# First FFN products of a hybrid encoder trunk taken slice by slice of the depth in eight PSUM banks, with new planned TensorE durations

## The chip, the cores and the metric

The kernel runs on one core of one Trainium2 chip. The metric is the time of one execution on the device in microseconds (us), lower is better. Engines are TensorE (PE; PEld is its weight load), VectorE (DVE), ScalarE (ACT), GpSimd (POOL) and SyncE (SP), which issues nearly all transfers.

## What is computed

A trunk of two layers, one sequence of 256 tokens of width 1024, all in float32. Each layer, with shift, scale and gate of every sub-layer computed from a vector c:

```python
x += 0.5 * g1 * SwiGLU(mod1(RMSNorm(x)))     # FFN 1
h  = mod2(RMSNorm(x)); p = h @ W_in
x += g2 * W_out(sum_b sigmoid(p_gate_b) * (mixer_b(p) @ P_b))   # three token mixers
x += 0.5 * g3 * SwiGLU(mod3(RMSNorm(x)))     # FFN 2

def modulate(h, shift, scale):
    return h * (1 + scale[:, None, :]) + shift[:, None, :]
def swiglu(h, wi, wo):
    gate, up = jnp.split(h @ wi, 2, axis=-1)
    return (jax.nn.silu(gate) * up) @ wo
```

Shift, scale and gate of all nine kinds are c (after SiLU) times `ada_w`, plus `ada_b`. The mixers are a dilated window attention, a 2-D neighbourhood attention and an RWKV-7 scan in both directions. The FFN is 2816 wide, 22 column blocks of 128 for the gate and 22 for the up half.

## The kernel before

Activations lie transposed, channels on the 128 partitions in eight slices (k = 0 to 7, `KT` = 8) and 256 tokens along the free axis. A float32 product is made from three float32r ones (`mm3`, lines 395 to 398): weights and activations are split into a high part (a cast, on ScalarE for weights) and a low part (the difference, on VectorE), and TensorE adds high x high, high x low and low x high in one PSUM bank.

**Who sets the order.** All instructions are written by a planner (`Order`, line 58). The stages are generators that say `yield on(engine, duration)`, `wait(event)` or `take(semaphore)`; the planner runs them in planned time, always the request that can start first, with a priority among equals. The order in which they come out is the order of each engine's queue on the chip. Planned durations are constants in the code: `MM` = 0.329 us for a triple of dense matmuls, 0.615 for eight small 64x64 ones, 1.14 for the reduction of an `ada_w` block, 1.45 for a transfer's issue. Buffers are counted too: `s_big` for 32 tiles of 4 KiB a partition, `s_pm` and `s_px` for 3 and 5 of the eight PSUM banks. The planner also models TensorE's clock (`clock`, line 103).

**The main stream.** `weights`, `weights_hi` and `weights_lo` (lines 331 to 364) load the weights in their order of use, 512 KB at a time, and split them in quarters; `dense` (line 440) runs the products. In `ffn` (line 785) each column block j takes gate and up (s = 0, 1) over all eight k, then `ffn_evac` (line 643) makes z on ScalarE and VectorE. Behind the first products, `ada` (line 492) loads further `ada_w` blocks at a planned pace (`FPACE` = 5 us from `FSTART` = 12 us on) and `ada_block` (line 457) reduces each against c on VectorE (line 460).

**The start.** The first sub-layer cannot use the main stream at once: its h needs the scale and the shift, eight `ada_w` blocks each, and the sum of squares of x. `first_loads` (line 721) loads, in the order of the list `FIRST`, `ada_w` blocks and halves of the weights of the first six column blocks (`NJ0` = 6; one half holds four k of one block, in runs of 2 KiB). The scale blocks are reduced on VectorE. The shift blocks of slices 0 to 6 are multiplied by c on GpSimd and added up on ScalarE (`first_shift`, line 697):

```python
nc.gpsimd.tensor_tensor(out=raw, in0=raw, in1=csb, op=OP.mult)
S_.activation(raw, raw, AF.Copy, scale=0.5, accum_out=modT[0][:, k:k + 1])
```

`first_put` (line 736) makes a slice of h: x times the reciprocal norm on VectorE, scale and shift on ScalarE, the cast on ScalarE, the low part on VectorE. `first_products` (line 756) takes six PSUM banks at once and runs the products in the order in which h and weight halves come, two k-halves a block. Then the other 16 column blocks follow from the main stream.

**After it.** The token mixer works with `ORDER` = "cabAgB": projections, the RWKV chain (inversion steps pX, pT at lines 1175 and 1186, the scan with pU at line 1296), the attentions, gates. The chains' small matmuls stand between dense ones; a chain's result `oC` (line 1435) is the last branch of the mixer. The columns of shift that `Stats.scale` (lines 511 to 527) writes are needed by the first products of the next sub-layer (`pearly`).

Of the kernel before, what the change touches and what calls it, by code (L numbers as in the profile page):

```python
# [16 lines left out]
KT = D // 128  # L17
# [12 lines left out]
NJ0, SHV = 6, (7,)  # L30
FIRST = ((0,), (0, 0), (1, 0), (2, 0), (3, 0), (4, 0), (1,), (5, 0), (2,), (0, 1), (1, 1), (3,), (2, 1), (3, 1), (4,), (4, 1), (5,), (5, 1), (6,), (7,))
# [4 lines left out]
LAT, MM = {"PE": 0.2, "ACT": 0.15, "DVE": 0.13, "SP": 0.0}, 0.329  # L36
# [21 lines left out]
class Order:  # L58
# [6 lines left out]
    def __init__(self):  # L65
        self.threads, self.free, self.cur, self.n = [], {}, None, 0
        self.dense, self.cols, self.thin, self.row, self.tab = None, {}, 0.0, 0, None

# [48 lines left out]
    def run(self):  # L117
        while self.threads:
# [11 lines left out]
            if kind == "on":  # L130
# [8 lines left out]
                if a == "PE":  # L139
                    if th is self.dense:  # L140
                        self.row += 1
                        if self.row >= BURST:
                            self.thin = 0.0
                    else:
                        self.row = 0
                        self.thin += b
                    b = self.clock(t, b, 0.98 if th is self.dense else 0.6) - t
# [11 lines left out]
def on(eng, dur, lat=None, tab=None):  # L159
    return ("on", eng, dur, LAT[eng if isinstance(eng, str) else eng[0]] if lat is None else lat, tab)  # L160
# [27 lines left out]
def trunk(ctx, tc, A, out):  # L188
# [404 lines left out]
    def rstd(st):  # L593
# [4 lines left out]
        yield on("PE", 0.6)  # L598
# [83 lines left out]
    w0 = {(j, q): Event() for j in range(NJ0) for q in range(2)}  # L682
    raws0 = {q: Event() for q in w0}

    def first_weights(j, q, raw):
        yield take(s_big, 2)
        hi, lo = (big("w0" + n, (128, 2, 512), F32R) for n in "hl")
        yield wait(raws0[j, q])
# [5 lines left out]
        w0[j, q].w = hi, lo  # L694
        od.set(w0[j, q])

    def first_shift(k, raw, got):
        yield wait(got)
        yield on("POOL", 2.3, 0.2)
        nc.gpsimd.tensor_tensor(out=raw, in0=raw, in1=csb, op=OP.mult)  # L700
        yield on("ACT", 1.05)
        S_.activation(raw, raw, AF.Copy, scale=0.5, accum_out=modT[0][:, k:k + 1])
        free_big()
        yield on("DVE", 0.07)
        V.tensor_add(modT[0][:, k:k + 1], modT[0][:, k:k + 1], ada_b[:, 0, k:k + 1])
        od.set(have1[k])

    def first_mod(k):
        if k in SHV:
            yield from ada_load(0, k, 1, False)  # L710
            yield from ada_load(0, 8 + k, 1, False)
            return
        yield take(s_big)
        raw, got = big("raw0", (128, D)), Event()
        yield on("SP", 1.45, 0.0)
        nc.sync.dma_start(raw, A["ada_w"][0, k])
        od.set(got, 2.0)
        od.spawn(first_shift(k, raw, got), 1)
        yield from ada_load(0, 8 + k, 1, False)

    def first_loads():

        for x in FIRST:
            if len(x) == 1:
                yield from first_mod(x[0])
                continue
            j, q = x
            yield take(s_big)
            raw = big("w0raw", (128, 2, 512))
# [26 lines left out]
    def first_products(ha):  # L756

        sems = [s_px] * min(NJ0, 4) + [s_pm] * (NJ0 - 4)
        for q in sems:
            yield take(q)  # L760
        ps0, za = [paux("pfirst", (128, 2, 256)) for _ in range(NJ0)], None
        at_ = {tuple(x): i for i, x in enumerate(FIRST)}
        jobs = sorted((max(at_[k,], at_[j, k // 4]), k, j) for k in range(KT) for j in range(NJ0))
        n, left0 = [0] * NJ0, [4 * NJ0] * 2
        for _, k, j in jobs:
            n[j] += 1
            if k == KT - 1 and za is None:
# [12 lines left out]
            left0[k // 4] -= 1  # L780
# [1127 lines left out]
```

## Time and profile before

| | us |
|---|---|
| median of three runs | 1587.9 |
| lowest, highest | 1582.06, 1589.01 |
| profiled execution, its own time | 1586.35 |
| its span, first to last instruction | 1584.6 |
| mean granted TensorE clock | 0.985 |

The profile is of one execution. Busy times of matmuls overlap, as each is counted until its result is written, so how far TensorE is from its peak is read from the distance of starts. A row of the timeline holds the start, the length, the engine, the line, what is written from what, the shape and, in brackets, the engine's idle time before it with what ended it; "x6" merges six like instructions. A row of the waits says who waited for what, then the total, the number of times and the longest. The granted clock is given as a share of 2.4 GHz.

### The profile page before, as it was taken

What the parts mean: (1) busy time and instruction counts of PE and PEld (TensorE: products, weight loads), DVE (VectorE), ACT (ScalarE), POOL (GpSimd) and SP (SyncE); (2) the same over time, 40 slices, a digit from 0 to 9 for tenths busy, and PEclk for the clock granted to TensorE, in tenths of its full rate; (3) what the DMA queues carried; (4) which work ended last, traced back from release to release, by engine and by line L of the source; (5) the groups of instructions that cost most, each with busy time, mean ns of one, the idle gap of its engine ahead of it and who ended that gap; (6) DMA issues with size and microseconds to landing.
All of it is one profiled execution on the core that took longest, in us unless ns stands there. A gap on an engine that the chain in (4) does not pass through costs nothing.

```text
span 1584.6 us, 36797 instructions
## 1 busy us (share of the span) xinstructions
PE 1533.1 (97%) x14518; PEld 1450.6 (92%) x14518; DVE 1311.7 (83%) x2938; ACT 897.0 (57%) x1854; POOL 21.3 (1%) x29
## 2 busy tenths in 40 slices
PE   3999999999999989999999999999999999999998
PEld 3999999988888889999999999998888987999997
DVE  7878889989888869997779877898888896888664
ACT  4655567576554447554565545676655445565554
POOL 3100000000000000000000000000000000000000
PEclk7999999999999989999999999999999999899999
DMA  8588864545464225888657876544446422467553
GB/s 310 188 293 272 284 230 163 180 130 198 140 230 140 74 80 174 277 287 273 226 200 272 285 266 203 185 159 155 160 159 232 168 102 68 136 202 274 184 184 127
DMA packets 91621, 311.61 MB, mean 197 GB/s; under 512 B 11444, under 2 KB 14772, under 8 KB 91448
## 3 DMA queue, kind: packets, MB, share of 16 engines
q1 hardware_dynamic: 91160, 309.15, 57.8%
q8 instruction: 114, 1.87, 0.5%
q14 instruction: 59, 0.48, 0.1%
q10 hardware_dynamic: 288, 0.10, 0.0%
HBM read 308.17 MB, written 1.05 MB: 195 GB/s over the span
## 4 chain that ended last, share of the span: by engine, by line
PE 88%; DMA 5%; DVE 4%; issue 1%; ACT 1%; SPq 0%; DVEq 0%; ACTq 0%
PE pmain L396 21%; PE pmain L397 20%; PE pmain L398 20%; DMA araw<-in_ada_w_dram 5%; PE pearly L396 2%; PE pearly L398 2%; PE pearly L397 2%; PE pX L1175 2%; PE pT L1186 2%; PE pG L1158 1%; PE pS L1488 1%; PE po L1528 1%; DVE wlo L361 1%; PE pmain L1645 1%; PE pmain L1647 1%
## 5 line engine op out<-in xcount | busy, mean ns | idle before, releaser
L352 ACT CAST whi<-wraw 128x512 fp32r<-128x512 f32 x836 | 511.9, 619 | 427.3 <-PE pmain L397 256.0
L361 DVE TENSOR_TENSOR wlo<-wraw,whi 128x512 fp32r<-128x512 f32 x836 | 571.7, 688 | 118.7 <-ACT whi L352 109.2
L396 PE MATMUL pmain<-h,whi 128*128 128x256 f32 x1872 | 539.2, 288 | 0.0
L398 PE MATMUL pmain<-h,wlo 128*128 128x256 f32 x1872 | 525.2, 281 | 1.1 <-DVE wlo L361 1.1
L397 PE MATMUL pmain<-h,whi 128*128 128x256 f32 x1872 | 525.2, 281 | 0.0
L396 PEld LDWEIGHTS pmain<-h,whi 128*128 128x128 f32 x1872 | 351.7, 188 | 13.3 <-issue 4.6
L398 PEld LDWEIGHTS pmain<-h,wlo 128*128 128x128 f32 x1872 | 352.2, 188 | 1.6 <-DVE wlo L361 1.6
L397 PEld LDWEIGHTS pmain<-h,whi 128*128 128x128 f32 x1872 | 352.3, 188 | 0.4
L460 DVE CUSTOM_DVE_ANT_0 araw<-araw,csb 128x1024 f32<-128x1024 f32 x137 | 169.0, 1235 | 47.6 <-DMA araw<-in_ada_w_dram 47.2
L398 PE MATMUL pmain<-z,wlo 128*128 128x256 f32 x704 | 198.2, 282 | 3.4 <-DVE wlo L361 3.3
L397 PE MATMUL pmain<-z,whi 128*128 128x256 f32 x704 | 197.9, 281 | 0.0
L396 PE MATMUL pmain<-z,whi 128*128 128x256 f32 x704 | 197.8, 281 | 0.0
L398 PEld LDWEIGHTS pmain<-z,wlo 128*128 128x128 f32 x704 | 132.6, 188 | 4.4 <-DVE wlo L361 4.2
L396 PEld LDWEIGHTS pmain<-z,whi 128*128 128x128 f32 x704 | 132.6, 188 | 0.0
L397 PEld LDWEIGHTS pmain<-z,whi 128*128 128x128 f32 x704 | 132.6, 188 | 0.0
L396 PE MATMUL pearly<-xh,whi 128*128 128x258 f32 x320 | 91.4, 286 | 0.0
L398 PE MATMUL pearly<-xh,wlo 128*128 128x258 f32 x320 | 90.4, 282 | 0.0
L397 PE MATMUL pearly<-xl,whi 128*128 128x258 f32 x320 | 90.2, 282 | 0.0
L397 PEld LDWEIGHTS pearly<-xl,whi 128*128 128x128 f32 x320 | 60.6, 189 | 0.0
L396 PEld LDWEIGHTS pearly<-xh,whi 128*128 128x128 f32 x320 | 60.4, 189 | 0.0
L398 PEld LDWEIGHTS pearly<-xh,wlo 128*128 128x128 f32 x320 | 60.3, 189 | 0.0
L419 ACT CAST z<-ffz 128x256 fp32r<-128x256 f32 x76 | 30.7, 405 | 40.3 <-DVE ffz L651 39.9
(306 smaller groups left out, 2459.2 us busy)
## 6 DMA issues: line engine op xcount, KB each, us to landing
wraw<-in_ffn_wi_dram SPq DMA_DIRECT2D x164, 512.0 KB, 4.9
araw<-in_ada_w_dram SPq DMA_DIRECT2D x137, 512.0 KB, 6.4
wraw<-in_ffn_wo_dram SPq DMA_DIRECT2D x88, 512.0 KB, 4.5
wraw<-in_w_in_dram SPq DMA_DIRECT2D x78, 512.0 KB, 3.7
wraw<-in_w_gb_dram SPq DMA_DIRECT2D x72, 512.0 KB, 4.2
wraw<-in_w_out_dram SPq DMA_DIRECT2D x16, 512.0 KB, 3.6
w0raw<-in_ffn_wi_dram SPq DMA_DIRECT2D x12, 512.0 KB, 9.8
raw<-in_ada_w_dram SPq DMA_DIRECT2D x7, 512.0 KB, 7.9
```

Source lines behind the costliest of these rows:

```text
L352: S_.copy(hi, part(q))
L361: V.tensor_tensor(lo, part(q), hi, op=OP.subtract)
L396: P.matmul(o, w[0], xh, start=first, stop=False)
L397: P.matmul(o, w[0], xl, start=False, stop=False)
L398: P.matmul(o, w[1], xh, start=False, stop=last)
L419: S_.copy(self.hi(k), src)
L460: V.tensor_tensor_reduce(out=raw, in0=raw, in1=csb, scale=0.5, scalar=0.0, op0=OP.mult, op1=OP.add, accum_out=modT[l][:, blk:blk + 1])
L1158: P.matmul(pp[b][:, i], BK[d][i // 2][hs, i % 2, c].rearrange("p a b -> p (a b)"), ar_view(d, i // 2)[hs, :, i % 2, cs_], start=True, stop ...
L1175: P.matmul(px[half(h), h // 2], G[half(h), h // 2, h % 2, 0:64], T[half(h), h // 2], start=True, stop=True)
L1186: P.matmul(pt[half(h), h // 2], X[half(h), h // 2], TT[half(h), h // 2], start=True, stop=True)
L1488: P.matmul(pS[e][:, t], qT[half(e), hp, t * 128:(t + 1) * 128], kT[half(e), hp], start=True, stop=True)
L1528: P.matmul(po[half(e)], vv[:, j, (2 * hp + e) * 64:(2 * hp + e + 1) * 64], pt_[:, 2 * e + j], start=j == 0, stop=j == 1)
```

## The change

`NJ0` becomes 8, and `FIRST`, `first_shift` and `first_mod` go. `first_loads` now goes by slices: for each k the scale block and the shift block, both reduced on VectorE through `ada_load`, and for each pair of slices four weight pieces, each with two k of four column blocks of one half (gate or up), in runs of 1 KiB. A piece takes three large buffers when it is issued. `first_put` waits for the scale first and makes x times scale times norm in one VectorE step, then adds the shift with the cast on ScalarE, and makes the low part with a three-operand VectorE step. `first_products` runs k by k, for each k over all eight blocks, with all eight banks open until the last k. In the planner a triple takes 0.354 instead of 0.329 us, the small steps get other durations and a form, and a change of form on TensorE costs `TURN` = 0.2 us. No instruction outside the start is added or removed; the order in every queue is planned anew.

```diff
--- before.py
+++ after.py
@@ -27,13 +27,13 @@
-NJ0, SHV = 6, (7,)
-FIRST = ((0,), (0, 0), (1, 0), (2, 0), (3, 0), (4, 0), (1,), (5, 0), (2,), (0, 1), (1, 1), (3,), (2, 1), (3, 1), (4,), (4, 1), (5,), (5, 1), (6,), (7,))
+NJ0 = 8
...
-LAT, MM = {"PE": 0.2, "ACT": 0.15, "DVE": 0.13, "SP": 0.0}, 0.329
+LAT, MM = {"PE": 0.2, "ACT": 0.15, "DVE": 0.13, "SP": 0.0}, 0.354
+TURN = 0.2
@@ -137,6 +138,9 @@ Order.run
                 if a == "PE":
+                    if th.req[5] != self.form:
+                        self.form = th.req[5]
+                        b += TURN
@@ -679,71 +684,52 @@
         yield from za.put(j, z)
         od.release(s_z, 3)
 
-    w0 = {(j, q): Event() for j in range(NJ0) for q in range(2)}
+
+
+    w0 = {(g, i): Event() for g in range(KT // 2) for i in range(NJ0 // 2)}
     raws0 = {q: Event() for q in w0}
 
-    def first_weights(j, q, raw):
-        yield take(s_big, 2)
-        hi, lo = (big("w0" + n, (128, 2, 512), F32R) for n in "hl")
-        yield wait(raws0[j, q])
+    def first_weights(g, i, raw):
+        hi, lo = (big("w0" + n, (128, 1024), F32R) for n in "hl")
+        yield wait(raws0[g, i])
         yield on("ACT", 0.94)
         S_.copy(hi, raw)
         yield on("DVE", 1.13)
         V.tensor_tensor(lo, raw, hi, op=OP.subtract)
         free_big()
-        w0[j, q].w = hi, lo
-        od.set(w0[j, q])
-
-    def first_shift(k, raw, got):
-        yield wait(got)
-        yield on("POOL", 2.3, 0.2)
-        nc.gpsimd.tensor_tensor(out=raw, in0=raw, in1=csb, op=OP.mult)
-        yield on("ACT", 1.05)
-        S_.activation(raw, raw, AF.Copy, scale=0.5, accum_out=modT[0][:, k:k + 1])
-        free_big()
-        yield on("DVE", 0.07)
-        V.tensor_add(modT[0][:, k:k + 1], modT[0][:, k:k + 1], ada_b[:, 0, k:k + 1])
-        od.set(have1[k])
-
-    def first_mod(k):
-        if k in SHV:
-            yield from ada_load(0, k, 1, False)
-            yield from ada_load(0, 8 + k, 1, False)
-            return
-        yield take(s_big)
-        raw, got = big("raw0", (128, D)), Event()
-        yield on("SP", 1.45, 0.0)
-        nc.sync.dma_start(raw, A["ada_w"][0, k])
-        od.set(got, 2.0)
-        od.spawn(first_shift(k, raw, got), 1)
-        yield from ada_load(0, 8 + k, 1, False)
+        w0[g, i].w = tuple(t.rearrange("p (j k c) -> p j k c", j=4, k=2) for t in (hi, lo))
+        od.set(w0[g, i])
 
     def first_loads():
 
-        for x in FIRST:
-            if len(x) == 1:
-                yield from first_mod(x[0])
-                continue
-            j, q = x
-            yield take(s_big)
-            raw = big("w0raw", (128, 2, 512))
-            yield on("SP", 1.45, 0.0)
-            nc.sync.dma_start(raw, A["ffn_wi"][0, 0, j].rearrange("p (s q c) -> p s q c", s=2, q=2)[:, :, q])
-            od.set(raws0[j, q], 2.0)
-            od.spawn(first_weights(j, q, raw), 2)
+        for k in range(KT):
+            yield from ada_load(0, 8 + k, 0, False)
+            yield from ada_load(0, k, 0, False)
+            for i in range(0 if k % 2 else NJ0 // 2):
+                yield take(s_big, 3)
+                raw = big("w0raw", (128, 1024))
+                yield on("SP", 1.45, 0.0)
+                j0, c0 = i // 2 * 4, i % 2 * 1024 + 128 * k
+                nc.sync.dma_start(raw.rearrange("p (j c) -> p j c", j=4),
+                                  A["ffn_wi"][0, 0, j0:j0 + 4].rearrange("j p c -> p j c")[:, :, c0:c0 + 256])
+                od.set(raws0[k // 2, i], 2.0)
+                od.spawn(first_weights(k // 2, i, raw), 2)
         od.set(e_w)
 
     def first_put(k, ha):
+        yield wait(have1[8 + k])
         yield take(s_z)
         t = small("ht")
-        yield on("DVE", 0.34)
-        V.tensor_mul(t, xT[:, k], first.r)
-        yield wait(have1[8 + k])
+        yield on("DVE", 0.4)
+        V.scalar_tensor_tensor(t, xT[:, k], modT[0][:, 8 + k:9 + k], first.r, op0=OP.mult, op1=OP.mult)
         yield wait(have1[k])
+        sh = modT[0][:, k:k + 1]
         yield on("ACT", 0.4)
-        S_.activation(t, t, AF.Identity, scale=modT[0][:, 8 + k:9 + k], bias=modT[0][:, k:k + 1])
-        yield from ha.put(k, t)
+        S_.activation(ha.hi(k), t, AF.Identity, bias=sh)
+        yield on("DVE", 0.396)
+        V.scalar_tensor_tensor(ha.lo(k), t, sh, ha.hi(k), op0=OP.add, op1=OP.subtract)
         od.release(s_z)
+        od.set(ha.ev[k])
@@ -754,32 +740,28 @@
         first.used()
 
     def first_products(ha):
-
-        sems = [s_px] * min(NJ0, 4) + [s_pm] * (NJ0 - 4)
-        for q in sems:
-            yield take(q)
-        ps0, za = [paux("pfirst", (128, 2, 256)) for _ in range(NJ0)], None
-        at_ = {tuple(x): i for i, x in enumerate(FIRST)}
-        jobs = sorted((max(at_[k,], at_[j, k // 4]), k, j) for k in range(KT) for j in range(NJ0))
-        n, left0 = [0] * NJ0, [4 * NJ0] * 2
-        for _, k, j in jobs:
-            n[j] += 1
-            if k == KT - 1 and za is None:
+        sems = [s_pm] * NPM + [s_px] * (NJ0 - NPM)
+        ps0, za = [], None
+        for k in range(KT):
+            if k == KT - 1:
                 yield take(s_big, 12)
                 za = Act("z", NJ)
-            yield wait(w0[j, k // 4])
-            hi, lo = w0[j, k // 4].w
-            for s in range(2):
-                c = slice(k % 4 * 128, k % 4 * 128 + 128)
-                if ha.ev[k].t is None or ha.ev[k].t > od.cur.t:
-                    yield wait(ha.ev[k])
-                yield on("PE", MM, 0.0)
-                mm3(ps0[j][:, s], (hi[:, s, c], lo[:, s, c]), ha.hi(k), ha.lo(k), n[j] == 1 and s == 0, n[j] == KT and s == 1)
-            if n[j] == KT:
-                od.spawn(ffn_evac(j, ps0[j], za, sems[j]), 1)
-            left0[k // 4] -= 1
-            if left0[k // 4] == 0:
-                free_big(2 * NJ0)
+            for i in range(NJ0 // 2):
+                yield wait(w0[k // 2, i])
+                hi, lo = w0[k // 2, i].w
+                for j in range(i // 2 * 4, i // 2 * 4 + 4):
+                    if ha.ev[k].t is None or ha.ev[k].t > od.cur.t:
+                        yield wait(ha.ev[k])
+                    if k == 0 and i % 2 == 0:
+                        yield take(sems[j])
+                        ps0.append(paux("pfirst", (128, 2, 256)))
+                    yield on("PE", MM, 0.0)
+                    mm3(ps0[j][:, i % 2], (hi[:, j % 4, k % 2], lo[:, j % 4, k % 2]), ha.hi(k), ha.lo(k),
+                        k == 0 and i % 2 == 0, k == KT - 1 and i % 2 == 1)
+                    if k == KT - 1 and i % 2 == 1:
+                        od.spawn(ffn_evac(j, ps0[j], za, sems[j]), 1)
+                if k % 2 == 1:
+                    free_big(2)
         return za
...
-            yield on("PE", 0.86)
+            yield on("PE", 0.86, form="64x128")
...
-                    yield on("PE", 0.435, 0.2 if i == 3 else 0.0)
+                    yield on("PE", 0.22, 0.2 if i == 3 else 0.0, form="64x128")
...
-                    yield on("PE", 0.615)
+                    yield on("PE", 0.48, form="64x64")
...
-                yield on("PE", 0.96)
+                yield on("PE", 0.87, form="64x128")
...
-                    yield on("PE", 0.65, 0.0)
+                    yield on("PE", 0.7, 0.0)
...
```

## Rows read from the trace of the kernel before

**Rows 1.** The page's first part: busy time, share of the span and instructions.
```profile
PE 1533.1 (97%) x14518; PEld 1450.6 (92%) x14518; DVE 1311.7 (83%) x2938; ACT 897.0 (57%) x1854; POOL 21.3 (1%) x29
```
**Rows 2.** Windows of 10 us: stretch, length, busy by engine, clock, DMA share, GB/s.
```profile
10.00:20.00 10.00, 2.56 (x10) 2.07 (x10) 8.10 (x12) 5.45 (x8) 3.05 (x2) 0.53 1.04 394
20.00:30.00 10.00, 3.26 (x13) 2.97 (x14) 10.00 (x12) 3.83 (x6) 6.07 (x3) 0.50 1.04 398
30.00:40.00 10.00, 6.53 (x39) 5.93 (x38) 9.58 (x13) 4.72 (x8) 3.00 (x2) 0.84 0.49 170
```
**Rows 3.** Waits of TensorE, 0 to 60 us: total us, times, longest.
```profile
PE pfirst L396 <- ACT h L419: 9.5, 2, 6.8
```
**Rows 4.** Timeline of all engines, 0 to 45 us: start, length, engine, line.
```profile
8.24 5.01 DVE L566 TENSOR_TENSOR sqacc<-sqacc,sq 128x256 f32<-128x256 f32 x6
...
9.00 2.38 POOL L700 TENSOR_TENSOR raw<-raw,csb 128x1024 f32<-128x1024 f32 x1 [8.57 <-DMA raw<-in_ada_w_dram]
...
27.52 3.13 POOL L700 TENSOR_TENSOR raw<-raw,csb 128x1024 f32<-128x1024 f32 x1 [2.68 <-DMA raw<-in_ada_w_dram]
...
28.32 3.41 DVE L460 CUSTOM_DVE_ANT_0 araw<-araw,csb 128x1024 f32<-128x1024 f32 x1
```
**Rows 5.** Timeline of VectorE, 36 to 51 us, away from GpSimd.
```profile
36.66 1.22 DVE L460 CUSTOM_DVE_ANT_0 araw<-araw,csb 128x1024 f32<-128x1024 f32 x1
...
38.06 0.15 DVE L705 TENSOR_TENSOR modT<-modT,c_ada_b 128x1 f32<-128x1 f32 x1
...
49.07 1.22 DVE L692 TENSOR_TENSOR w0l<-w0raw,w0h 128x1024 fp32r<-128x1024 f32 x1
50.26 0.43 DVE L421 TENSOR_TENSOR h<-ht,h 128x256 fp32r<-128x256 f32 x1
50.60 1.22 DVE L460 CUSTOM_DVE_ANT_0 araw<-araw,csb 128x1024 f32<-128x1024 f32 x1
```
**Rows 6.** Timeline of TensorE: runs of first products, then the first streamed product.
```profile
28.34 0.41 PE L398 MATMUL pfirst<-h,w0l 128*128 128x256 f32 x1
...
30.90 0.37 PE L398 MATMUL pfirst<-h,w0l 128*128 128x256 f32 x1
...
50.18 0.28 PE L396 MATMUL pfirst<-h,w0h 128*128 128x256 f32 x1
...
55.13 0.28 PE L396 MATMUL pfirst<-h,w0h 128*128 128x256 f32 x1
...
69.12 0.28 PE L396 MATMUL pmain<-h,whi 128*128 128x256 f32 x1
```
**Rows 7.** Timelines, 217 to 225 us: last shift column written, first product that uses it.
```profile
217.06 0.17 DVE L526 TENSOR_TENSOR xl<-modT,xh 128x8 fp32r<-128x8 f32 x1
...
224.32 0.28 PE L396 MATMUL pearly<-xh,whi 128*128 128x258 f32 x1
```
**Rows 8.** Waits of TensorE from 60 us to the end: total us, times, longest.
```profile
PE pgi L1408 <- DVE gsq L1403: 3.2, 2, 1.6
PE pmain L396 <- ACT oC L1435: 2.8, 2, 1.4
PE pvar L1390 <- ACT gsq L1382: 2.3, 2, 1.1
```
**Rows 9.** One window at the end of the first layer's token mixer, columns as in rows 2.
```profile
573.80:584.10 10.30, 7.58 (x31) 6.75 (x32) 5.16 (x13) 2.82 (x7) 0.00 (x0) 0.50 0.00 0
```
**Rows 10.** Groups of TensorE instructions by form: count, busy us, mean ns, idle before.
```profile
L1175 PE MATMUL pX<-txw,G 64*64 64x64 f32 x768 | 32.4, 223 | 1.6 <-DVE txw L1238 1.4
L1186 PE MATMUL pT<-txw 64*64 64x64 f32 x768 | 32.3, 223 | 0.0
```
**Rows 11.** Timeline of TensorE around one small step among dense matmuls, 566 us.
```profile
566.56 0.28 PE L398 MATMUL pmain<-h,wlo 128*128 128x256 f32 x1
566.77 0.68 PE L1296 MATMUL pU<-txw 64*64 64x64 f32 x16
...
567.60 0.28 PE L397 MATMUL pmain<-o,whi 128*128 128x256 f32 x1
```

More of the change, by code (lines that the diff above doesn't have):

```diff
@@ L67, in __init__ @@
         self.dense, self.cols, self.thin, self.row, self.tab = None, {}, 0.0, 0, None
+        self.form = None
     def spawn(self, gen, prio, dense=False):
@@ L155, in run, with on @@
             self.step(th)
-def on(eng, dur, lat=None, tab=None):
-    return ("on", eng, dur, LAT[eng if isinstance(eng, str) else eng[0]] if lat is None else lat, tab)
+def on(eng, dur, lat=None, tab=None, form=None):
+    return ("on", eng, dur, LAT[eng if isinstance(eng, str) else eng[0]] if lat is None else lat, tab, form)
 def wait(ev):
@@ L597, in rstd @@
         p = paux("pss")
-        yield on("PE", 0.6)
+        yield on("PE", 0.9)
         for t in range(2):
@@ L1026, in kk_norm @@
                     pss = paux("pkk", (128, S))
-                yield on("PE", 0.5)
+                yield on("PE", 0.44, form="128x32")
                 head_sum(pss, d, kq, d == 1)
@@ L1061, in finish @@
                     p = paux("pinv", (128, 2, S))
-                    yield on("PE", 0.434)
+                    yield on("PE", 0.48, form="64x128")
                     head_bcast(p, d, q, KK)
@@ L1103, in finish @@
                     pbs = paux("pbs", (128, S))
-                yield on("PE", 0.5)
+                yield on("PE", 0.44, form="128x32")
                 head_sum(pbs, d, RKV[d, 1], d == 1)
@@ L1119, in finish @@
                     p = paux("pbon", (128, 2, S))
-                    yield on("PE", 0.434)
+                    yield on("PE", 0.48, form="64x128")
                     head_bcast(p, d, q, rows)
@@ L1183, in invert @@
                     pt = paux("pT", (128, 4, 64))
-                    yield on("PE", 0.615)
+                    yield on("PE", 0.48, form="64x64")
                     for h in range(8):
@@ L1246, in values @@
                 p = paux("pBT", (128, 4, 64))
-                yield on("PE", 0.22)
+                yield on("PE", 0.25, form="64x128")
                 for i in range(4):
@@ L1254, in values @@
             p = paux("pvt", (128, 4, 64))
-            yield on("PE", 0.648)
+            yield on("PE", 0.48, form="64x64")
             for h in range(8):
@@ L1263, in values @@
             p = paux("pMV", (128, 4, 64))
-            yield on("PE", 0.615)
+            yield on("PE", 0.48, form="64x64")
             for h in range(8):
@@ L1285, in scan @@
                     p = paux("pAS", (128, 4, 64))
-                    yield on("PE", 0.615)
+                    yield on("PE", 0.48, form="64x64")
                     for h in range(8):
@@ L1293, in scan @@
                 p = paux("pU", (128, 4, 64))
-                yield on("PE", 0.615)
+                yield on("PE", 0.48, form="64x64")
                 for h in range(8):
@@ L1305, in scan @@
                     p = paux("pS1", (128, 4, 64))
-                    yield on("PE", 0.615)
+                    yield on("PE", 0.48, form="128x64")
                     for h in range(8):
@@ L1321, in scan @@
                 p = paux("pY", (128, 4, 64))
-                yield on("PE", 1.275 if ST is not None else 0.615)
+                yield on("PE", 1.05 if ST is not None else 0.48, form="128x64")
                 for h in range(8):
@@ L1387, in post @@
             p = paux("pvar", (128, 8))
-            yield on("PE", 0.8)
+            yield on("PE", 0.9)
             for hp in range(4):
@@ L1524, in attend @@
                 po = paux("po", (128, S))
-                yield on("PE", 0.96)
+                yield on("PE", 0.87, form="128x64")
                 for j in range(2):
```

## Prediction

> **What bounds the kernel now.** I read the share of each engine first: TensorE holds matmuls for 97% of the span, the next engine (VectorE) 83% [rows 1]. So a gain must either give TensorE back idle time or time at the low clock; work taken from another engine is worth nothing by itself. Next I looked at where TensorE is not full. The stretches of the first 40 us show it busy for 2.6, 3.3 and 6.5 of 10 us, at a granted clock of 0.53, 0.50 and 0.84, while VectorE is busy for 8.1, 10.0 and 9.6 [rows 2]; 0.50 is the lower of the clock's two levels, 1.2 of 2.4 GHz. In the waits of that stretch the biggest one is the first product waiting for a slice of h, 9.5 us in two pieces [rows 3]. So the start is bound by VectorE, and the rows say why: whenever GpSimd multiplies an `ada_w` block by c, a VectorE instruction beside it grows. The reduction of line 460 takes 3.41 us beside a GpSimd product and 1.22 us alone [rows 4, 5]; six additions of squares take 5.01 us with one GpSimd product of 2.38 us over them [rows 4].
>
> The first products end and the streamed ones begin at 69.12 us [rows 6]. From there TensorE is almost never short: the nine lines of its waits behind that point add up to about 21 us, and three of them belong to the end of the token mixer, with 3.2, 2.8 and 2.3 us [rows 8].
>
> **The start, part by part.** *Matmuls.* Nothing is added or dropped: eight of the 22 column blocks of the first FFN product go in the first part instead of six, and 14 instead of 16 are streamed. At the high clock 42 starts in a row take 55.13 - 50.18 = 4.95 us, 0.118 us each; at the low one 12 starts take 30.90 - 28.34 = 2.56 us, 0.213 us each [rows 6]. A streamed block is 16 x 3 = 48 matmuls, 5.66 us. Before, the first FFN product ends at about 69.1 + 16 x 5.66 = 159.7 us. After, it ends at T + 14 x 5.66 = T + 79.2, where T is the end of the first part. The change therefore gains 80.5 - T, and T has to be found.
>
> *GpSimd out, VectorE in.* Seven GpSimd products and seven ScalarE reductions go; all 16 `ada_w` blocks are reduced on VectorE. A block costs 38.06 - 36.66 = 1.40 us from its start to the next instruction but one, its small corrections included [rows 5]. Sixteen of them are 22.4 us, of which about seven, 9.8 us, are new on VectorE; what goes with GpSimd is the blocking. Low parts of the weight pieces: 50.26 - 49.07 = 1.19 us each [rows 5], 16 pieces instead of 12, 19.0 us. Two small steps for each of the eight slices: one takes 50.60 - 50.26 = 0.34 us now [rows 5]; the new forms read one operand more, and I take 0.40 us, an estimate, so 6.4 us. VectorE starts this after the squares: without GpSimd 8.24 + 5.01 - 2.38 = 10.9 us [rows 4]. Then 10.9 + 22.4 + 19.0 + 6.4 = 58.7 us if it never waits. In 10 to 40 us it was idle for 2.3 us [rows 2]; I add that, 61.0 us. The last slice is then ready and TensorE needs 48 x 0.118 = 5.7 us for it: T = 66.7, rounded to 67.
>
> *TensorE beside it.* 8 x 48 = 384 matmuls are 45.3 us at the high clock. VectorE needs (58.7 - 10.9) / 8 = 6.0 us for a slice, TensorE 5.7 us, so the slices follow each other almost without idle time, and TensorE ends just behind VectorE. If the first slice starts about 17 us (10.9 plus two reductions and two or three weight pieces), TensorE alone would end at 62.3 us, some 2 us later with a low clock at the beginning. It is no second bound, but it is close. The products of a slice wait in TensorE's order for that slice of h and its weight pieces; only later slices are queued behind them, and nobody else needs TensorE there.
>
> *Loads.* 32 pieces of 0.524 MB and x of 1.05 MB are 17.8 MB; at the 394 to 398 GB/s of 10 to 30 us [rows 2] that is 45 us, against 61 us of VectorE. They are hidden as long as space for them comes free: each weight piece now takes three of the 32 large buffers at its issue, and a pair of slices gives its eight back only when TensorE has used the second one. Before, DMA fell to 170 GB/s in 30 to 40 us [rows 2] because buffers were full; this can come again. A weight piece comes in runs of 1 KiB instead of 2 KiB, which no row shows. From below that costs nothing (pieces of 2 and of 4 KiB runs share the full rate); from above, if a run cost the same time whatever its size, a piece would take 2.6 us instead of 1.3, 16 x 1.3 = 21 us more. I take nothing, the row being nearer; the other end is a rival. SP issues nothing else in this stretch, so no other queue is delayed by the new order; the streamed weights queue behind these loads as they did.
>
> *Banks.* All eight PSUM banks are held until the last slice. The streamed product waits for bank 0 of them, which is emptied while the second half of the last slice (2.8 us) still runs on TensorE; its chain of one ScalarE and two VectorE steps of about 0.4 us each [rows 5] fits. If VectorE is behind then, up to 2 us show; that is inside the range.
>
> *What is late next.* The shift columns for the early products of the mixer are ready at 217.2 us and first used at 224.3 us, 7.1 us later [rows 7]. The use moves forward by 13 us. Their loads are paced in planned time, 24 blocks in steps of 5 us beginning 12 us behind T; planned time ran fast before (a triple was planned at 0.329 us and takes 3 x 0.118 = 0.354), so 127 planned us were 137 real ones. With 0.354 they come 10 us earlier besides the 2 us of T. About 5 us of cover stay: I cost it at nothing, and at 4 us if the pace doesn't move.
>
> So the start gains 80.5 - 67 = 13.5 us; I book 13.
>
> **The rest of the order.** No instruction changes there; the order of each queue is made anew. Dense triples are planned 7.6% longer. An excursion to small matmuls, the 16 of pU, takes from the dense matmul before it (566.56) to the second one after it (567.60) 1.04 us, less two dense starts 0.80 us [rows 11]; it was planned at 0.615 and is now 0.48 + 0.2 + 0.2 = 0.88. So the plan was optimistic for TensorE everywhere, and its chains through VectorE and ScalarE were covered with more dense work than they needed. That shows twice: few waits within the mixer, and a mixer chain that ends after the dense work has run out, with idle time and a clock of 0.50 for 10.3 us [rows 8, 9]. With true durations less dense work stands between two steps of a chain; the chain ends earlier, but has less cover. At most the end is worth its idle time, (3.2 + 2.8 + 2.3) / 2 = 4.2 us, and half of the other 6.1 us at the low clock, 3 us, or 7.2 us in each of two layers, about 14 us. I take about a fifth of that, 3 us, because thinner cover takes some back, and VectorE, the next engine [rows 1], does not get faster.
>
> **Sum.** The profiled execution took 1586.35 us (span 1584.6): 1586.35 - 13 - 3 = 1570.4, say 1570. It lies 1.6 us under the median of 1587.9 us, inside the spread of the three runs, so the same figure stands against the median. About 0.5% (7.9 us) is what a measurement here tells from no change: faster means under 1580.0, slower over 1595.8.
>
> **Rivals.** *Low clock, the slower end.* Slices come at VectorE's pace; if TensorE stays at 0.213 us a start for the whole part, it takes 384 x 0.213 = 82 us from 17 us on, T = 99, a loss of 18.5 us: 1586.35 + 18.5 - 3 = 1602. It decides from T = 80.5, that is if 141 of the 384 starts or more run low beyond what I booked (13.5 / 0.095). Against it: a TensorE at half speed is never idle here, since 10.2 us a slice exceeds VectorE's 6.0, and in the trace the start went from 0.213 to 0.118 us after an unbroken run of low starts [rows 6]. For it: the clock there is 0.50 in 20 to 30 us [rows 2], so the part begins low. The Trainium skill, "TensorE: Matmul & The Clock Gate", section "HAM oscillation — how this bites in real kernels", speaks against the change here: a loop that waits for new data at each K tile makes the array go back to its low clock at each of them. By that rule the result is this rival's; the row bears it out only in part, as the low clock is there but ended under unbroken work. Chance 0.07.
>
> *The loads.* With the upper price of the 1 KiB runs, or the same lost to full buffers, the loads end 21 us later, about 71 us, and T is near 80: the start gains nothing, 1583. For it speaks the fall to 170 GB/s [rows 2]; against it that the loads need 45 of the 61 us, so that some 13 us may be lost before they decide. Chance 0.14.
>
> *Thin cover.* pX and pT alone are 768 matmuls each, 16 to a step: 96 steps of the inversion chain [rows 10]. If TensorE now waits 0.3 us at each, that is 29 us: 1586.35 - 13 + 29 = 1602; from 0.14 us a step it eats the start's gain. Against it: VectorE's planned costs are near its real ones (a weight piece 1.13 us planned, 1.19 real), so the cover should just do. Chance 0.14.
>
> *The mixer's end goes too.* All 14 us of it: 1586.35 - 13 - 14 = 1559. Chance 0.13.
>
> **Chances and range.** My forecast has the remaining 0.52, with a range of its own of 1561 to 1579. Faster: 0.50 of it, all of the last rival, and a few hundredths of the loads and of thin cover, 0.67. Slower: the low clock and half of thin cover with a rest of the forecast, 0.15. The same: 0.18. The range leaves out the far ends of thin cover and the low clock above and little below: 1556 to 1592.
>
> **What would show it.** Right: no GpSimd product; line 460 never over 1.3 us in the first 65 us; first streamed product between 64 and 70 us; each slice's 48 matmuls close behind the one before. Wrong: starts of 0.213 us behind 30 us (low clock); TensorE or ScalarE waiting for a weight load in 20 to 60 us (loads); waits of TensorE for VectorE in 240 to 560 us well above now; or the first early product of the mixer waiting for the shift columns. The end of the mixer without a stretch at 0.50 would show that more was won than I book.

## The result and the profile after

The changed kernel takes 1594.41 us (median of 8 runs, 1588.43 to 1599.34), the kernel before 1584.74 us (8 runs, 1581.3 to 1589.01): a ratio of 1.0061, with an interval of 1.0037 to 1.0084. It is slower by some 0.6%, where 1570 was forecast. The profiled execution took 1599.34 us (span 1597.6), 4.9 us above the median; that of before took 1586.35. The two are 13.0 us apart, 3.3 more than the medians, and what is summed from the traces below is larger by that.

The page's first part, as in [rows 1]:

```profile
PE 1540.4 (96%) x14518; PEld 1453.6 (91%) x14518; DVE 1308.3 (82%) x2973; ACT 881.0 (55%) x1807; POOL 2.4 (0%) x22
```

GpSimd's work fell from 21.3 to 2.4 us. TensorE has the same number of matmuls and 7 us more busy time, VectorE and ScalarE have a little less: this row alone does not say where the time went.

The start, in the windows of [rows 2] and one more (columns as there):

```profile
10.00:20.00 10.00, 3.87 (x14) 3.09 (x15) 9.79 (x17) 5.11 (x7) 0.00 (x0) 0.57 1.06 382
20.00:30.00 10.00, 10.00 (x68) 10.00 (x67) 10.00 (x20) 4.80 (x6) 0.00 (x0) 0.75 1.07 374
30.00:40.00 10.00, 10.00 (x87) 10.00 (x86) 9.93 (x20) 4.70 (x6) 0.00 (x0) 1.00 1.07 370
...
50.00:60.00 10.00, 10.00 (x87) 10.00 (x86) 8.55 (x15) 5.15 (x8) 0.00 (x0) 1.00 0.68 251
```

From 20 us on TensorE is full, and from 30 us on at the high clock; VectorE is full up to 50 us. Three rows more answer [rows 4 to 6]: the reductions of the first 65 us and the low parts of h there (count, shortest/median/longest in ns, first and last start), and the first streamed product:

```profile
L465 DVE CUSTOM_DVE_ANT_0 araw<-araw,csb x16: 1215/1218/1222, 11.2 to 53.9; 128x1024 f32<-128x1024 f32 x16
```

```profile
L730 DVE SCALAR_TENSOR_TENSOR h<-ht,modT,h x8: 474/478/478, 18.7 to 56.9; 128x256 fp32r<-128x256 f32 x8
```

```profile
67.28 0.28 PE L401 MATMUL pmain<-h,whi 128*128 128x256 f32 x1
```

No reduction of the start takes longer than 1.22 us any more, and the first part ends at 67.3 us. So the start did what the change says.

**Where the time went.** The table gives the start of the first matmul of each stage, read from the timelines of TensorE, in us; what follows a mixer is the product with `W_out`. The last column is e9_no_landing_wait, the changed kernel in the same order with one wait taken away (below).

| first matmul of | before | after | after minus before | e9 |
|---|---|---|---|---|
| streamed part of FFN 1's first product | 69.1 | 67.3 | -1.8 | 67.7 |
| FFN 1's second product | 161.2 | 151.5 | -9.7 | 148.1 |
| mixer 1 (`pearly`) | 224.3 | 218.9 | -5.4 | 210.5 |
| mixer 1's last branch (`oC`) | 577.6 | 572.6 | -5.0 | 559.7 |
| what follows mixer 1 | 592.4 | 583.9 | -8.5 | 571.0 |
| FFN 2 | 614.9 | 606.6 | -8.3 | 593.7 |
| FFN 2's second product | 740.5 | 740.7 | +0.2 | 720.3 |
| layer 2, FFN 1 | 804.4 | 804.4 | 0.0 | 782.7 |
| its second product | 930.8 | 936.3 | +5.5 | 908.1 |
| mixer 2 | 996.1 | 1002.6 | +6.5 | 971.0 |
| mixer 2's last branch | 1349.4 | 1364.6 | +15.2 | 1321.8 |
| what follows mixer 2 | 1363.9 | 1375.9 | +12.0 | 1333.3 |
| last matmul | 1578.0 | 1590.7 | +12.7 | 1547.6 |

The gain of the start (13.1 us in e9) should stand at the second product; 9.7 are left there, 5.4 at the mixer, and it is gone at 740 us. What is lost comes in the FFNs (3.4 of the 13.1, then stretches that are longer by 4.3, 8.5, 5.5 and 1.0: 22.7 us up to 1002.6) and in mixer 2 (8.7 us); at the end of each mixer 3.5 and 3.2 us are won.

The waits of TensorE over the whole run, of after and then of before, and those of VectorE for `ada_w` blocks in the same order (total us, times, longest):

```profile
PE pmain L403 <- DVE wlo L366: 17.9, 19, 2.0
PE p L1204 <- DVE m L1199: 5.7, 11, 1.5
PE pX L1157 <- DVE txw L1220: 4.6, 11, 1.2
```

```profile
PE pmain L398 <- DVE wlo L361: 4.4, 5, 1.6
PE p L1222 <- DVE m L1217: 3.7, 4, 1.0
```

```profile
DVE araw L465 <- DMA araw<-in_ada_w_dram: 75.2, 49, 4.8
```

```profile
DVE araw L460 <- DMA araw<-in_ada_w_dram: 47.2, 39, 3.2
```

The wait that grew most on TensorE is the one of the streamed products for the low part of a weight quarter: 17.9 us instead of 4.4. On VectorE, which makes the low parts, it is the wait for the transfer of an `ada_w` block; of its 75.2 us in after, 57.2 lie in the FFNs and 11.0, in four stops, in mixer 2. One such place in FFN 2, on VectorE, then its transfer's issue on SP, then the chain of waits, then TensorE's first row behind its stop (start, length, what):

```profile
681.71 0.42 DVE L426 TENSOR_TENSOR z<-ffz,z 128x256 fp32r<-128x256 f32 x1
685.30 1.23 DVE L465 CUSTOM_DVE_ANT_0 araw<-araw,csb 128x1024 f32<-128x1024 f32 x1 [3.17 <-DMA araw<-in_ada_w_dram]
686.45 0.08 DVE L465 DVE_READ_ACCUMULATOR2_ANT modT<- 128x1 f32 x1
686.45 1.89 DVE L366 TENSOR_TENSOR wlo<-wraw,whi 128x512 fp32r<-128x512 f32 x3
```

```profile
678.47 0.42 SPq L492 DMA_DIRECT2D araw<-in_ada_w_dram  x1
```

```profile
678.47 6.81 DMA araw<-in_ada_w_dram
...
686.53 0.62 DVE wlo L366
...
687.19 0.55 PE pmain L403
687.74 0.21 PE pmain L401
```

```profile
687.19 0.55 PE L403 MATMUL pmain<-h,wlo 128*128 128x256 f32 x1 [1.94 <-DVE wlo L366]
```

The block is issued at 678.47 and lands 6.81 us later. VectorE works through its queue in order; its reduction comes up at 682.1, so it stands for 3.17 us, and behind the reduction wait three low parts that TensorE needs next. TensorE runs dry for 1.94 us, and the next matmuls start 0.21 us apart, the low clock's distance [rows 6]. In the plan a block lands 2.0 us after the 1.45 us of its issue, so 3.45 us after the issue begins. On the chip the paced blocks take this long (issue to landing, shortest/median/longest), after and then before:

```profile
DMA to landing us min/median/max: 4.5/6.3/7.8
```

```profile
DMA to landing us min/median/max: 5.1/6.4/8.2
```

So the plan was short by some 3 us at the median for both kernels; before, VectorE stood too, but TensorE seldom noticed.

### The profile page after: what moved, and what is told of

Its sections match the earlier page's. It is cut to its first block, busy times and chain, and to the rows that moved or that the text cites. A ratio compares the mean times of both kernels' runs of the same rounds, so it can differ in the third digit from the quotient of the medians.

```text
span 1597.6 us, 36768 instructions
## 1 busy us (share of the span) xinstructions
PE 1540.4 (96%) x14518; PEld 1453.6 (91%) x14518; DVE 1308.3 (82%) x2973; ACT 881.0 (55%) x1807; POOL 2.4 (0%) x22
## 4 chain that ended last, share of the span: by engine, by line
PE 66%; DVE 15%; DMA 12%; issue 4%; ACT 1%; SPq 0%; DVEq 0%; ACTq 0%
PE pmain L401 16%; PE pmain L403 15%; PE pmain L402 15%; DMA araw<-in_ada_w_dram 9%; DVE wlo L366 5%; PE pearly L401 2%; PE pearly L403 2%; PE pearly L402 2%; DMA wraw<-in_ffn_wi_dram 2%; DVE araw L465 2%; PE pfirst L402 1%; PE pfirst L403 1%; PE pfirst L401 1%; DMA bt<-in_bt_dram 1%; DVE G L1145 1%
## 5 line engine op out<-in xcount | busy, mean ns | idle before, releaser
L357 ACT CAST whi<-wraw 128x512 fp32r<-128x512 f32 x828 | 505.6, 619 | 440.1 <-PE pmain L402 266.6
L366 DVE TENSOR_TENSOR wlo<-wraw,whi 128x512 fp32r<-128x512 f32 x828 | 564.5, 688 | 113.8 <-ACT whi L357 107.8
L401 PE MATMUL pmain<-h,whi 128*128 128x256 f32 x1840 | 535.5, 291 | 0.1
L403 PE MATMUL pmain<-h,wlo 128*128 128x256 f32 x1840 | 519.8, 282 | 11.0 <-DVE wlo L366 10.7
L402 PE MATMUL pmain<-h,whi 128*128 128x256 f32 x1840 | 517.6, 281 | 0.0
L401 PEld LDWEIGHTS pmain<-h,whi 128*128 128x128 f32 x1840 | 348.0, 189 | 18.4 <-issue 9.6
L403 PEld LDWEIGHTS pmain<-h,wlo 128*128 128x128 f32 x1840 | 348.2, 189 | 15.0 <-DVE wlo L366 14.9
L402 PEld LDWEIGHTS pmain<-h,whi 128*128 128x128 f32 x1840 | 348.4, 189 | 0.4
L465 DVE CUSTOM_DVE_ANT_0 araw<-araw,csb 128x1024 f32<-128x1024 f32 x144 | 175.2, 1220 | 75.4 <-DMA araw<-in_ada_w_dram 75.2
```

Source lines behind the costliest of these rows:

```text
L357: S_.copy(hi, part(q))
L366: V.tensor_tensor(lo, part(q), hi, op=OP.subtract)
L401: P.matmul(o, w[0], xh, start=first, stop=False)
L402: P.matmul(o, w[0], xl, start=False, stop=False)
L403: P.matmul(o, w[1], xh, start=False, stop=last)
L465: V.tensor_tensor_reduce(out=raw, in0=raw, in1=csb, scale=0.5, scalar=0.0, op0=OP.mult, op1=OP.add, accum_out=modT[l][:, blk:blk + 1])
```

## The experiments

The theory from here on: **late blocks**, VectorE standing for `ada_w` blocks that land later than planned, with low parts of weights queued behind. The first rival: the **start**, or the first blocks behind it, costs later what it won. The second: **durations**, a plan made with the longer triple or the new small steps simply has too thin a cover. Ratios are to the kernel before on the same chip, each with its 95% interval. Before took 1582.62 to 1584.74 us beside the different runs, so a difference of two of their times is good to some 2 us.

**Each half alone.** The new start with the old durations (e3):

```diff
-LAT, MM = {"PE": 0.2, "ACT": 0.15, "DVE": 0.13, "SP": 0.0}, 0.354
-TURN = 0.2
+LAT, MM = {"PE": 0.2, "ACT": 0.15, "DVE": 0.13, "SP": 0.0}, 0.329
-                    yield on("PE", 0.48, form="64x64")
+                    yield on("PE", 0.615)
...
```

> The new first part (slices of the depth, eight banks, no GpSimd) with the old planned durations. Theory 'the order takes it back': the start keeps its 13 us to the end, about 1572 us against about 1585 before, first streamed product near 67 us, and the FFN parts behind it as long as before. Rival 'the start itself costs later' (weights or reductions that come late behind it): 1585 or more, with the loss already in the first FFN's output product.

Measured 1621.41 us, 1.0243 (1.0229 to 1.0256): the theory's 1572 us did not come, and the loss is not where the rival put it. The FFN stages keep the gain: TensorE waits 3.2 us in all for low parts, and FFN 1's second product starts at 147.0 us. But mixer 1 takes 48.3 us longer than before. Two windows in it, of this kernel:

```profile
400.00:440.00 40.00, 33.62 (x234) 27.62 (x233) 31.33 (x72) 17.18 (x43) 0.00 (x0) 0.87 0.42 143
440.00:480.00 40.00, 28.04 (x358) 23.36 (x357) 30.56 (x91) 19.12 (x47) 0.00 (x0) 0.90 0.55 186
```

TensorE has 33.6 and 28.0 of 40 us there, where before had 39.0 and 39.2, and just ahead (360 to 400 us) it ran 439 matmuls where before ran 336. That looks like dense work spent too early and a chain that has none left beside it. This wasn't tested; what in the new start makes that order from the old durations stays open.

The old start with the new durations (e4):

```diff
-LAT, MM = {"PE": 0.2, "ACT": 0.15, "DVE": 0.13, "SP": 0.0}, 0.329
+LAT, MM = {"PE": 0.2, "ACT": 0.15, "DVE": 0.13, "SP": 0.0}, 0.354
+TURN = 0.2
-                    yield on("PE", 0.615)
+                    yield on("PE", 0.48, form="64x64")
...
```

> The old first part with the new planned durations of TensorE. Theory 'the order takes it back': some 20 us slower than before, about 1605 us, with longer waits of TensorE for weight low parts in the FFNs (17.9 us in the changed kernel, 4.4 before) and for small mixer steps. Rival 'the start itself costs later': about the time of before, 1585 us.

Measured 1600.90 us, 1.0108 (1.0092 to 1.0125). The start's rival falls: without the new start a loss of 17 us is there. TensorE's waits show it:

```profile
PE pmain L404 <- DVE wlo L367: 15.9, 16, 2.1
```

**The plan told the landing (e1).** One constant of the changed kernel:

```diff
-        od.set(got, 2.0)
+        od.set(got, 6.0 if paced else 2.0)
```

> The changed kernel with one planned figure changed: a paced block of ada_w is planned to have landed 6.0 instead of 2.0 us after its issue; its reduction on VectorE so stands further back. Theory 'VectorE waits in order for a late block, with weight low parts queued behind it' (75 us of such waits in the changed kernel, 47 before): these waits fall below 20 us, TensorE's waits for weight low parts fall from 18 to about 4 us, the time falls by 15 to 20 us to some 1577 us. Rival 'VectorE has too much to do for each block because the pace of the loads is faster in real time': waits for landing fall, but the time stays within 5 us of 1594.

Measured 1553.21 us, 0.9815 (0.9801 to 0.9828): 41 us less than after (39 by the ratios), twice what was expected, and faster than both kernels. The wait of streamed products for low parts has all but gone; here is what leads the list of waits behind the start, and that wait:

```profile
PE pX L1157 <- DVE txw L1220: 3.6, 7, 1.3
...
PE pmain L403 <- DVE wlo L366: 0.3, 1, 0.3
```

**The pace instead (e2).** Blocks 7.6% further apart, as the triple is longer, with the landing left at 2.0:

```diff
-PACE, START = 7, 110
-FPACE, FSTART = 5, 12
+PACE, START = 7.53, 118
+FPACE, FSTART = 5.38, 12.9
```

> The changed kernel with the planned pace of the ada_w loads stretched by 7.6% (5.38 and 7.53 us for 5 and 7, starts 12.9 and 118 for 12 and 110), so that their real pace is that of before. Theory 'late landing': little, 0 to 5 us off 1594, as each block is still planned to land 2 us after issue. Rival 'the real pace is too fast for VectorE': the FFN parts are as long as before again, some 20 us less, about 1575.

Measured 1576.77 us, 0.9960 (0.9947 to 0.9974). It gives back some 17 us: the rival's figure, not the theory's. The waits for low parts and for blocks are:

```profile
PE pmain L403 <- DVE wlo L366: 8.9, 13, 1.6
```

```profile
DVE araw L465 <- DMA araw<-in_ada_w_dram: 72.5, 52, 4.5
```

VectorE stands for blocks about as long as in after (75.2 us), and TensorE waits half as long for low parts. So a late block alone does not cost the time; it costs where VectorE has no time to catch up before its low parts are needed, and a wider pace gives it some. That last step is a reading of the two lines and wasn't measured by itself.

**The wait alone, in the same order (e9).** A new landing makes a new order, so e1 might win by that. Here the order is that of after (the instructions of every engine and the transfers' issues come in the same order in both traces), and a reduction takes as long (1.22 us), but the paced ones read and write tiles that are always there:

```diff
-        V.tensor_tensor_reduce(out=raw, in0=raw, in1=csb, scale=0.5, scalar=0.0, op0=OP.mult, op1=OP.add,
+        V.tensor_tensor_reduce(out=scr if paced else raw, in0=csb if paced else raw, in1=csb, scale=0.5, scalar=0.0, op0=OP.mult, op1=OP.add,
```

> The changed kernel in its own order of every queue; only the paced reductions of ada_w blocks on VectorE read and write resident tiles instead of the block, so that they wait for no transfer, which still runs (what is computed for shift, scale and gate from the second sub-layer on is left out by this). Theory 'VectorE stands waiting for a late block, with weight low parts queued behind': TensorE's waits for low parts fall from 18 to 5 us or less and the time to about 1565 to 1575 us, without any new order. Rival 'it was the new order that won in the run with the later planned landing, not the landing': stays within 5 us of 1594.

Measured 1555.56 us, 0.9826 (0.9812 to 0.9841): the 39 us (37 by the ratios) come with the wait alone, more than the 20 to 30 that were expected. The edit also lets a block's buffer come free before the block has landed; but SyncE's waits at the issue of blocks hardly change (15.0 us in after, 11.2 here), so that is not where the time comes from. From 615 to 960 us, that is FFN 2 and layer 2's FFN 1, the window of before, of after and of this kernel:

```profile
615.00:960.00 345.00, 341.63 (x2884) 340.81 (x2883) 290.12 (x596) 191.17 (x372) 1.07 (x9) 1.00 0.75 255
```

```profile
615.00:960.00 345.00, 333.51 (x2759) 330.48 (x2758) 280.67 (x579) 182.98 (x356) 1.08 (x9) 0.99 0.74 248
```

```profile
615.00:960.00 345.00, 345.00 (x2920) 344.99 (x2919) 289.38 (x580) 196.74 (x370) 1.07 (x9) 1.00 0.75 259
```

TensorE is idle for 11.5 us in after, for 3.4 in before and for none here, with as much VectorE work and DMA traffic as before. After starts 161 matmuls fewer there than this kernel, 19.0 us at 0.118 us each; what the idle time doesn't explain of it is mostly slower starts behind the stops, as in the piece shown above. This is the run on which the theory rests. By the table above, the 43.1 us between the two profiled executions lie in the FFNs for 27.6 and in the mixers for 15.5: blocks are paced through these too.

**Dose.** The planned landing at 0 (e10) and at 4 us (e11), else as e1:

```diff
-        od.set(got, 2.0)
+        od.set(got, 0.0 if paced else 2.0)
```

> The changed kernel with a paced ada_w block planned to land 0 instead of 2.0 us after its issue: its reduction stands some 1.4 weight quarters further forward on VectorE. Theory 'late landing': VectorE's waits for blocks grow from 75 to 120 us or more, TensorE's waits for low parts with them, 1620 us or more. Rival 'any other order is better than the one of the change': below 1590.

Measured 1706.96 us, 1.0773 (1.0754 to 1.0792), with these waits of TensorE and of VectorE:

```profile
PE pmain L403 <- DVE wlo L366: 75.6, 46, 3.3
```

```profile
DVE araw L465 <- DMA araw<-in_ada_w_dram: 191.2, 79, 4.3
```

```diff
-        od.set(got, 2.0)
+        od.set(got, 4.0 if paced else 2.0)
```

> The same with 4.0 us. Theory 'late landing': between 1594 (at 2.0) and 1553 (at 6.0); blocks really land 4.5 to 7.8 us after issue, of which 1.45 are planned on top, so most of it is won already: 1555 to 1570.

Measured 1573.43 us, 0.9935 (0.9917 to 0.9954), just above what was expected. Planned landings of 0, 2, 4 and 6 us give 1707, 1594, 1573 and 1553 us. At 4 VectorE waits 2.5 us for blocks in the whole run, so the last 20 us are not that wait: by the stage starts they lie in the two mixers, +6.3 and +6.5 us against before where e1 has -4.0 and -4.9. They are another order of the mixers; why it is worse was not followed up. An order alone can so move the time by 20 us, and the dose alone would not show the cause; e9, which keeps the order, does.

**Which duration uncovered it.** After with the old triple (e5), then after with the old small steps (e6):

```diff
-LAT, MM = {"PE": 0.2, "ACT": 0.15, "DVE": 0.13, "SP": 0.0}, 0.354
+LAT, MM = {"PE": 0.2, "ACT": 0.15, "DVE": 0.13, "SP": 0.0}, 0.329
```

> The changed kernel with only the dense triple planned at 0.329 us again; small steps and the form change stay new. Theory 'the true dense duration makes the blocks come faster in real time and uncovers their landing': the FFN parts are as short as before again, so about 1575 us. Rival 'the small steps and the form change set it off': stays near 1594.

Measured 1576.59 us, 0.9964 (0.9947 to 0.9980).

```diff
-TURN = 0.2
+TURN = 0.0
-                    yield on("PE", 0.48, form="64x64")
+                    yield on("PE", 0.615)
...
```

> The changed kernel with the old durations of small steps and no form change; the dense triple stays at 0.354 us. Theory 'the true dense duration uncovers the landing': as slow as the changed kernel in the FFN parts, 1590 to 1600 us. Rival 'the small steps set it off': 1575 us or less. The mixer of the first layer is open: with old durations of both kinds behind the new start it grew by 48 us.

Measured 1592.59 us, 1.0058 (1.0039 to 1.0077). It is the triple: with 0.329 TensorE waits 0.7 us for low parts, though VectorE still waits for blocks, 43.5 us in all:

```profile
PE pmain L403 <- DVE wlo L366: 0.7, 2, 0.4
```

```profile
DVE araw L465 <- DMA araw<-in_ada_w_dram: 43.5, 40, 2.5
```

With the old small steps and 0.354 (e6) it waits 13.3, with those and 0.329 (e3) 3.2. A triple planned at 0.329 and run at 0.354 gives every engine beside it 7.6% more time than the plan counts on; that this slack took up the late blocks is read from these pairs and from e2. e5 has the start's gain at FFN 1's second product (147.7 us), but loses 4.6 us in that product, at whose end TensorE waits 2.9 us for the sum of squares and for no low part, and its mixer 2 takes 7.6 us longer than before.

**The landing told to the old durations.** Before with 6.0 (e7), and the new start on old durations with 6.0 (e8); both edits are that of e1.

```diff
-        od.set(got, 2.0)
+        od.set(got, 6.0 if paced else 2.0)
```

> The kernel before with the landing of a paced ada_w block planned at 6.0 instead of 2.0 us. Theory 'the old, too short TensorE durations left enough ready weights to cover late blocks': little is won, 0 to 10 us, 1574 to 1584. Rival 'late blocks cost the same with either set of durations': 30 us or more are won, below 1555.

> The new first part with the old planned durations of TensorE and the landing at 6.0 us. It tells what the measured durations are worth once blocks are not late. Theory 'with the landing right, true durations shorten the chains and the mixer's end': 1565 to 1575, some 15 us slower than with the new durations and the same landing (1553), with a stretch at the low clock at the end of each mixer. Rival 'the durations are worth nothing by themselves': within 5 us of 1553. The 48 us that the first mixer lost with old durations and landing at 2.0 may come back here; then it is 1600.

Measured 1595.31 us, 1.0077 (1.0060 to 1.0094), and 1593.85 us, 1.0060 (1.0041 to 1.0078). Both are slower than the theories said. With the old durations the truth about the landing wins nothing: the FFNs of e7 are as long as those of before in layer 1 (within 0.5 us each), and its mixers are 8.6 and 4.0 us longer. In e8 the mixers are 15.9 and 8.8 us longer, which eats the start; the stretch at the low clock at their ends, which was expected there, did not come. So of the two corrections to the plan each one alone costs 13 and 17 us against before (e7, e4), and both with the new start win 30, of which 13 are the start's. The old start with both was not run. Why the mixers come out 4 to 48 us longer in some of these orders (e3, e5, e7, e8, e11) stays open.

**Weights too (e12).** After with 6.0 and with the landing of the streamed weights at 3.5:

```diff
-            od.set(raws[i, h], 2.0)
+            od.set(raws[i, h], 3.5)
```

> The changed kernel with the landing of blocks at 6.0 and of streamed weights at 3.5 instead of 2.0 us. VectorE waits 143 us for high parts of weights in the run with 6.0 alone, without TensorE waiting for it. Theory 'cover is enough there': within 4 us of 1553. Rival 'weights are late too': 5 us or more less.

Measured 1555.14 us, 0.9822 (0.9806 to 0.9838), the same as e1: telling the plan more of the weights' landing wins nothing more.

## Why the prediction was wrong

**The start, 13 us booked: right.** At FFN 1's second product e1 and e9, where no block is late, stand 13.1 us ahead of before. T was to be 67 and is 67.3. The engine that sets it is another, though: VectorE was to end at 61.0 and writes its last low part at 56.9 + 0.5 = 57.4; its idle 2.3 us did not come (VectorE is idle for 0.3 us from 10 to 40 us). TensorE was to end by itself at 62.3 or 2 us later; with its first start at 18.2 us, 45.3 us at the high clock and 3.8 us lost to the low one and a first stop it ends at 67.3. Two terms were off by 3 to 5 us, one each way, and cancelled: that T came out to 0.3 us was luck.

**Its low-clock rival: did not come.** The granted clock is 0.57, 0.75 and 1.00 in three windows from 10 us on; the starts at the low level's distance are over within some 7 us of the first product. The Trainium skill, "TensorE: Matmul & The Clock Gate", section "HAM oscillation — how this bites in real kernels", has the array return to the low clock where the wait for data is longer than the products of a K tile, a condition that the prediction left out; here, where TensorE is the slower of the two and does not run dry between slices, the trace does not show the return, which agrees with that section.

**The loads: no bound.** They ran at 370 to 382 GB/s up to 50 us and ended in time: behind its first stop TensorE waits for nothing up to 67.3 us. A piece in runs of 1 KiB did cost more than a block, by an estimate from 348 against 411 GB/s (shown at the end) some 0.2 us, 3.7 us for 16, where nothing was booked; it stayed hidden. The fall to 170 GB/s in 30 to 40 us [rows 2] did not come back; the rate falls only behind these loads, to 68 GB/s from 60 to 67.3 us.

**Shift columns: right.** The last one is written from 212.2 to 212.4 us and first used at 218.9: 6.5 us of cover, where about 5 were expected.

**The rest of the order, -3 us booked: this is the step that failed.** The medians say 1594.41 - 1584.74 + 13.1 = +22.8 us, the profiled execution 12.7 + 13.1 = +25.8. With the wait for late blocks alone taken away (e9) they say 1555.56 - 1582.62 + 13.1 = -14 us: that wait costs more than all that the change won elsewhere. The idle end of the mixers, on which the -3 rested [rows 8, 9], went: 3.5 and 3.2 us are won there, 6.7 of the 14 us and more than the 3 booked. That the true durations won them is not shown, as e8 has mixer ends of the same length, some 11.3 us, with the old ones. What was missing is the other side. I argued that the blocks behind the start "come 10 us earlier" and cost nothing, and looked at their columns' due time only; I did not ask what stands behind a block in VectorE's queue, though its transfer's planned time of 2.0 us is in the code and the trace of before has 47.2 us of VectorE waiting for just these transfers. That row points at the missing term, which the prediction put at nothing: stops that were covered as long as the triple was planned 7.6% too short, which the change corrects. With the true triple TensorE's waits for low parts went from 4.4 to 17.9 us, and with the old one in the same kernel they are 0.7 (e5).

**The thin cover, 1602 at 0.14: right in direction, wrong in place.** It put 0.3 us at each of 96 inversion steps. The waits at pX are 4.6 us in all; 17.9 us are at the FFNs' weights. The reason I gave against it was that VectorE's planned costs are near its real ones. That holds for its instructions (1.22 us against 1.14) and not for what it waits for. Of my signs, "waits of TensorE for VectorE in 240 to 560 us" looked at the wrong stretch: the five stretches of 22.7 us lie outside it, and so does mixer 2 with its 8.7.

## What to carry to other kernels

If a planner writes the order, its errors cover each other: making one duration true can cost time until the next one is true as well (here the durations alone cost 17 us and the landing alone 13, and both with the new start win 30, 13 of them by the start). When a plan's slack is removed, list every wait that already stands on an engine that works in order, with what is queued behind it, even where nobody waits for it today. A transfer's landing belongs in the plan as measured under load in that stage.

## What the runs showed of the hardware

A 512 KB transfer amid the stream of weights (248 to 259 GB/s from 615 to 960 us) landed 4.5 to 7.8 us after its issue in after (3.4 to 9.2 in e1), with a median of 6.3, and the median depends little on the order: 5.3 us in e10, 5.7 in e1 and e11, 5.9 in e5, 6.0 in e9, 6.4 before. What share of it is other traffic wasn't measured. Weight pieces in runs of 1 KiB move more slowly than blocks in runs of 4 KiB. The rate of after in 40 equal slices from 10 to 65 us:

```profile
GB/s 370 347 351 387 402 414 409 358 349 346 350 378 411 402 414 351 349 348 349 368 401 417 408 372 351 348 352 369 397 409 411 411 188 30 36 316 191 219 20 0
```

It swings between some 350 and 410 GB/s, in the rhythm in which four weight pieces and four `ada_w` blocks (runs of 4 KiB) are issued. The packets of a low stretch, 21 to 24 us, and of a high one, 16 to 18.5 us, tell which is which: all packets of the first are under 2 KB, and all but 31 of the second lie between 2 and 8 KB.

```profile
DMA packets 1050, 1.04 MB, mean 348 GB/s; under 512 B 32, under 2 KB 1050, under 8 KB 1050
```

```profile
DMA packets 282, 1.03 MB, mean 411 GB/s; under 512 B 31, under 2 KB 31, under 8 KB 282
```

So in this stretch runs of 1 KiB moved at 348 GB/s and runs of 4 KiB at 411.
